# Decoder layer on one core: three small loads held behind a weight's cast, attention and decay steps shifted, cross-attention's scores in float32r parts

## The chip, the cores and the metric

The kernel runs on one core of one Trainium2 chip, in one launch. The metric is the device time of one execution in microseconds (us). The core has five engines that run side by side: TensorE (PE in the profile, with its weight loads as PEld), VectorE (DVE), ScalarE (ACT), GpSimd (POOL) and SyncE (SP). Each engine runs its own instructions strictly in order, and waits on semaphores for the others. Loads and stores are issued by SP, ACT or POOL and carried out by 16 DMA engines.

## The reference

One hybrid decoder layer on 256 tokens of width 2048, all in float32:

```
x = x + 0.5 * swiglu(rms_norm(x), ffn1)                     # inner width 5632
p = rms_norm(x) @ w_in;  q, k, v, p_rwkv, gates = split(p)
y_attn = sliding_window_attention(q, k, v, sinks)           # 16 heads, 4 kv heads, window 128
y_rwkv = rwkv7_time_mix(p_rwkv, ...)                        # 16 heads of 64
x = x + (gate_a * (y_attn @ w_pa) + gate_r * (y_rwkv @ w_pr)) @ w_out
x = x + cross_attention(rms_norm(x), rms_norm(mem)) @ w_o   # 4 heads of 128, 256 memory rows
x = rms_norm(x + 0.5 * swiglu(rms_norm(x), ffn2))
```

The attention has a learned sink per head, which enters the maximum and the denominator of the softmax: `p = e / (sum(e) + exp(sink - m))`. In the RWKV part a decay and a rate come from sigmoids of two small products, and the state is updated token by token; the kernel computes it in blocks, with the inverse of a triangular matrix per head and block. In cross-attention the scores are `s = q km^T / sqrt(128)` for each of 4 heads, then a softmax over the 256 rows of the memory. Every matrix product has to keep float32's accuracy, more or less.

## The kernel before

Nearly all of the time goes to products of 256 tokens with the weights. A weight tile (128 rows, 2 blocks of rows, 512 columns) is loaded by SP into a buffer `raw`. ACT casts it to the shorter type float32r (`hi`, line 345), DVE subtracts to get the rest (`lo`, line 346), and PE runs three float32r matmuls of 128x512 in place of one float32 matmul: hi times the activations' hi (line 438), lo times hi (439) and hi times the activations' lo (440). I call these the big matmuls. The two feed-forward blocks also save products by sums and differences of weight tiles (lines 365 to 371).

Everything else is woven between the big matmuls. Each such piece of work is a Python generator: `attend` for sliding-window attention, `decay_and_rate`, `removal_keys`, `substitute`, `invert` and `chain` for RWKV, `look_up` for cross-attention, `late_vectors` for small constants. After every six big matmuls `product` calls `bg.tick()`, which advances each generator at the head of its group by one step, up to its next `yield`. `yield from idle(n)` skips n ticks. So the numbers in `idle` set where a piece's instructions enter the program. After that a scheduler may still move instructions of an engine forward or back where data allow; `tc.issue_after(i)` forbids moving ahead of the instruction i. `newest["act"]` is the latest cast of a weight.

The parts that the change touches:

- `late_vectors` loads three small arrays from POOL: later gains (32 KB, line 266), the RWKV vectors (41.5 KB, line 267) and the sinks (8 KB, line 268), and derives `nk_k` and `ok_a` from the second on DVE (lines 270, 271). It waits 60 ticks first, but its loads have nothing to wait for.
- `attend(kvs, qb)` runs six times: scores (line 179, PE), maximum (964, DVE), exponentials (970, ACT, one for each head), denominators (977 to 979, DVE), scaling (980, DVE), transposes by PE (187), a copy `pt` (996, ACT) and the product with the values (179). `kvs` are the key-value heads, `qb` the block of 128 queries.
- `decay_and_rate` has two halves of eight sigmoids each (line 1109, ACT), and pauses after each. `tok` (line 907, ACT) is the scaled result of a projection, which PE then transposes (187).
- `substitute` inverts small blocks row by row and stores them twice with POOL (`xd` line 1254, `xe` 1256), the second after a transposing copy on ACT (1255). `invert` loads them as `xb` and `xu` (lines 1341, 1345), and joins the blocks by small matmuls (1351), at its last level through a copy `n2_` (1388).
- `look_up` multiplies `qc` and `km` for cross-attention's scores (line 1693), in float32. The profile shows each such matmul as two records.

Of the kernel before, what the change touches and what calls it, by code (L numbers as in the profile page):

```python
# [15 lines left out]
P = 128  # L16
# [126 lines left out]
def decoder_layer(ctx: ExitStack, tc: tile.TileContext, a: dict, out: bass.AP):  # L143
# [19 lines left out]
    def f32(x):  # L163
        return x.bitcast(F32)
# [28 lines left out]
    def idle(n):  # L193
        for _ in range(n):
            yield
# [67 lines left out]

    def late_vectors():
        yield from idle(60)
        pool.dma_start(gains[:], a["g_later"])
        pool.dma_start(rv[:], a["v_rwkv"])
        pool.dma_start(sinks[:], a["attn_sinks"].broadcast_to([P, 16]))
        yield from idle(20)
        dve.tensor_scalar(nk_k[:], k_k, -1.0, None, ALU.mult)  # L270
        dve.tensor_scalar(ok_a[:], k_a, -1.0, 1.0, ALU.mult, ALU.add)
# [384 lines left out]
    def feats(tok, cols=(0, P, 2 * P, 3 * P)):  # L656


        b = two()[:].rearrange("p a (c t) -> p (a c) t", t=T)
        turn(  # L660
            (b[:, i, t * P : (t + 1) * P], tok[:, t, col : col + P])
            for t in (1, 0) for i, col in enumerate(cols)
        )
        return b[:, : len(cols)]
# [227 lines left out]
    with tc.tile_pool(name="mx", bufs=1, reuse_waits="tile") as sp:  # L892
        aligned(sp)

        def t4(name, shape=(P, 4, T), dt=F32):
            return sp.tile(list(shape), dt, tag="t4", name=name, bufs=N4)
# [14 lines left out]


        def to_features(tok, dst, name):
            last = act.copy(dst[:], feats(tok))
            if name == "q0":
                with tc.issue_after(last.ins):
                    act.activation(junk_t[:, :1], ones[:, :1], AF.Exp)
            yield
            bg.seen.add(name)
# [4 lines left out]
        def attend(kvs, qb):  # L924
# [27 lines left out]
            def each(name):  # L952
                return stat.tile([P, n], F32, tag=name, name=name)
# [2 lines left out]
                return v[:].rearrange("p (e k c) -> p e k c", e=2, k=nk)  # L956

            m, nm, es, den = (each(name) for name in ("m", "nm", "es", "den"))
            b3 = b[:].rearrange("p e (c w) -> p (e c) w", w=w)
            s3 = s[:].rearrange("p e c w -> p (e c) w")  # L960
            sink = sinks[:, 4 * kvs[0] : 4 * kvs[0] + n].rearrange(
# [18 lines left out]
            dve.tensor_tensor(  # L980
                s3, s3, den[:].unsqueeze(2).to_broadcast([P, n, w]), ALU.mult
            )
            yield from idle(5 if nk == 2 and kvs[0] else 4)
            pt = t4("pt", (P, 2, 4, P))
            b = two()
            turn(
# [97 lines left out]
        def decay_and_rate():  # L1084
            yield from wait_for("small")
            yield from wait_for("attn")
            wa = t4("wa", (P, RW))
            pool.dma_start(wa[0:64, :], W["rwkv_w2"])
            pool.dma_start(wa[64:128, :], W["rwkv_a2"])
            act.activation(xwa[0:64, :], xwa[0:64, :], AF.Tanh)  # L1090
            act.activation(xg, xg, AF.Sigmoid)
            yield from idle(3)
            for h in range(2):
                cs.append(t4("cs"))
                aa.append(t4("aa"))
                for q in (0, 2):
                    b = two()
                    by_turns(
                        (
                            b[:, e, i * T : (i + 1) * T],  # L1100
                            wa[64 * e : 64 * e + 64, (4 * h + q + i) * P : (4 * h + q + i + 1) * P],
                            xwa[64 * e : 64 * e + 64, :],
                        )
                        for i in range(2) for e in (1, 0)
                    )
                    for i in range(2):
                        for e, (dst, bias) in enumerate(((cs[h], w0), (aa[h], a0))):
                            c = 4 * h + q + i
                            rates = act.activation(
                                dst[:, q + i, :], b[:, e, i * T : (i + 1) * T], AF.Sigmoid,  # L1110
                                bias=bias[:, c : c + 1],
                            )
                yield from idle(4)
            for h in range(2):
                for c in range(4):
                    dve.tensor_tensor_scan(
                        cs[h][:, c, :], keep2, cs[h][:, c, :], 0.0, ALU.mult, ALU.add
                    )
                    if c % 2:
                        yield  # L1120
                c3 = halves(cs[h])
                mid = stat.tile([P, 8], F32, tag="mid", name="mid")
                dve.tensor_copy(mid[:], c3[:, :, 63])
                dve.tensor_tensor(
                    c3, c3, mid[:].unsqueeze(2).to_broadcast([P, 8, P]), ALU.subtract
                )
                dec.append(stat.tile([P, 4], F32, tag="dec", name="dec"))
                dve.tensor_tensor(dec[h][:], cs[h][:, :, 127], mid[:, 1:8:2], ALU.add)
                yield
                ee.append(t4("ee", (P, 8, P)))  # L1130
                e0.append(stat.tile([P, 8], F32, tag="e0", name="e0"))
                with tc.issue_after(rates.ins):
                    act.activation(dec[h][:], dec[h][:], AF.Exp, scale=-DECAY)
                    act.activation(e0[h][:], mid[:], AF.Exp, scale=DECAY)
                    act.activation(ee[h][:], c3, AF.Exp, scale=-DECAY)
                yield
                act.activation(cs[h][:], cs[h][:], AF.Exp, scale=DECAY)
                yield
            bg.seen.add("decay")
# [95 lines left out]
        def substitute():  # L1235
            yield from idle(4)
            dl = t4("dl", (P, 32, 32))
            for i in range(4):
                q = slice(32 * i, 32 * i + 32)
                pool.dma_start(dl[q], ld[q, :, q].rearrange("t h s -> h t s"))  # L1240
            xt = t4("xt", (P, 32, 32))
            pool.memset(xt[:], 0.0)
            pool.memset(xt[:].rearrange("p u t -> p (u t)")[:, 0 : 32 * 32 : 33], 1.0)
            yield from idle(14)
            tmp = t4("tmp", (P, 32, 32))
            for t in range(1, 32):
                dve.tensor_tensor(
                    tmp[:, :t, :t], xt[:, :t, :t],
                    dl[:, t, :t].unsqueeze(1).to_broadcast([P, t, t]), ALU.mult,
                )  # L1250
                yield
                dve.tensor_reduce(xt[:, :t, t], tmp[:, :t, :t], AX.X, ALU.add)
                yield from idle(1 + t // 20)
            pool.dma_start(xd[:].rearrange("i h u t -> (i h) u t"), xt[:])
            act.copy(tmp[:96], xt[:96].rearrange("p u t -> p t u"))
            pool.dma_start(xe[:].rearrange("i h t u -> (i h) t u"), tmp[:96])
            yield from idle(2)
            bg.seen.add("inverse")
# [68 lines left out]
        def invert(h):  # L1327
# [58 lines left out]
                for c, n in both  # L1386
            )
            act.copy(n2_[low].rearrange("p c n t -> p c (n t)"), b[low])
            yield
            b = two()  # L1390
            several(
                (b[low, c, n * 64 : n * 64 + 64], xu[low, c, n, :], n2_[low, c, n, :])
# [279 lines left out]
                bg.spawn("mem", memory())  # L1672


        km, vm, qc = t4("km"), t4("vm", (P, 2, 512)), t4("qc")
        bg.until(lambda: hasattr(nm_, "r"))
        tok = scaled(product(nm_.x, W["w_cross_kv"]), nm_.r)
        bg.spawn("feat", to_features(tok, km, "km"))
# [5 lines left out]
        def look_up(t):  # L1684
            yield from wait_for("qc")
            ts = slice(t * P, (t + 1) * P)
            s = t4("sm")
            m = stat.tile([P, 4], F32, tag="m", name="m")
            nm = stat.tile([P, 4], F32, tag="nm", name="nm")
            den = stat.tile([P, 4], F32, tag="den", name="den")  # L1690
            b4 = two()[:].rearrange("p a (h m) -> p (a h) m", h=2)
            for h in range(4):
                pe.matmul(b4[:, h], qc[:, h, ts], km[:, h, :], start=True, stop=True)
            dve.tensor_reduce(m[:], b4, AX.X, ALU.max)
            dve.tensor_scalar(nm[:], m[:], -SC, None, ALU.mult)
            for h in range(4):
                act.activation(
                    s[:, h, :], b4[:, h, :], AF.Exp, scale=SC, bias=nm[:, h : h + 1],
                    accum_out=den[:, h : h + 1],
                )  # L1700
            yield
            dve.reciprocal(den[:], den[:])
            for i in range(4):
                dve.tensor_scalar(s[:, i, :], s[:, i, :], den[:, i : i + 1], None, ALU.mult)
            yield
            b = two()
            turn(
                (b[:, mb, i * P : (i + 1) * P], s[:, i, mb * P : (mb + 1) * P])
                for i in (3, 2, 1, 0) for mb in range(2)
            )  # L1710
            for mb in range(2):
                act.copy(pt[mb][:, :, ts], b[:, mb].rearrange("p (h t) -> p h t", h=4))
            yield
# [141 lines left out]
```

## Time and profile before

| what | value |
|---|---|
| median of 3 runs | 2218.01 us (2217.72 to 2218.32) |
| the profiled execution's own time | 2218.37 us |
| its span (first to last instruction) | 2216.6 us |
| mean granted TensorE clock | 0.999 |
| busy: PE / PEld / DVE / ACT / POOL | 2202.8 / 1816.7 / 1761.8 / 1197.5 / 72.2 us |
| moved by DMA | 433.31 MB, mean 195 GB/s |

The busy times are of the profiled execution. Its own time exceeds its span by 1.8 us, which lies around the first and the last instruction. PE's records overlap: a big matmul lasts 0.39 us in the trace, and the next one starts 0.23 us after it. So distances from start to start tell more about PE than durations. In a row of the timeline stand the start, the duration, the engine, the line, the operation with its output and inputs, the number of instructions that follow each other, and in square brackets the idle time ahead of it with the instruction that ended it. In a row of the chain stand the start and the duration of a piece of the chain of work that ended last.

Stages in the trace: the first feed-forward block until about 690 us, then the input projection with attention at about 765 to 825, RWKV's decay at about 845 to 855, its inversion and chain until 1200, the output projection, cross-attention at about 1440 to 1470, and the second feed-forward block until the end.

### The profile page before, as it was taken

The page shows a single profiled execution, that of the slowest core. Times are in us where ns is not written, and L with a number is a line of the kernel's source. Part 1 is how long each engine was busy: PE and PEld are TensorE (multiplying, and loading weights), DVE is VectorE, ACT ScalarE, POOL GpSimd, SP SyncE. Part 2 cuts the span into 40 slices and gives each one's busy share as a digit, 9 for nine tenths or more (in the row PEclk, how much of TensorE's full clock was granted, in tenths as well). Part 3 has the DMA queues.
Part 4 walks back from the last instruction along what each step waited for, and adds up shares of the span by engine and source line. Part 5 has one row for each costly group of instructions (what it writes and reads, how often), then busy time and mean ns, then how long its engine had stood idle before and what let it go on. Part 6 is the DMA issues. An engine that isn't in the chain of part 4 may idle for free.

```text
span 2216.6 us, 28327 instructions
## 1 busy us (share of the span) xinstructions
PE 2202.8 (99%) x10774; PEld 1816.7 (82%) x10774; DVE 1761.8 (79%) x2053; ACT 1197.5 (54%) x1447; POOL 72.2 (3%) x141
## 2 busy tenths in 40 slices
PE   9999999999999999999999999999999999999998
PEld 7888888888888877888888888888888888888886
DVE  8988988898887477888556676558888988898887
ACT  6555555555555557534445455556555555555554
POOL 1000000000000000010400000000000000000000
PEclk9999999999999999999999999999999999999999
DMA  7665665565656545677714765557565565565564
GB/s 261 205 219 194 204 207 192 190 209 190 209 178 220 171 128 155 214 230 222 206 54 150 235 218 202 184 171 262 193 206 185 196 209 191 188 209 196 203 207 153
DMA packets 220536, 433.31 MB, mean 195 GB/s; under 512 B 13952, under 2 KB 16336, under 8 KB 220400
## 3 DMA queue, kind: packets, MB, share of 16 engines
q1 hardware_dynamic: 213200, 410.70, 56.0%
q0 software_dynamic: 6624, 20.14, 2.9%
q8 instruction: 84, 1.38, 0.2%
q10 hardware_dynamic: 576, 0.66, 0.1%
q14 instruction: 52, 0.43, 0.1%
HBM read 419.00 MB, written 12.45 MB: 195 GB/s over the span
## 4 chain that ended last, share of the span: by engine, by line
PE 96%; DVE 1%; DMA 1%; ACT 1%; issue 1%; SPq 0%; POOLq 0%; POOL 0%; ACTq 0%; DVEq 0%
PE acc L438 21%; PE acc L439 21%; PE acc L440 21%; PE two L438 9%; PE two L439 9%; PE two L440 9%; PE two L187 2%; PE two L179 1%; DMA raw<-in_ffn_w_up_dram 1%; DVE lo L346 1%; PE two L1351 0%; PE acc L1488 0%; PE acc L1453 0%; PE acc L1470 0%; PE acc L1351 0%
## 5 line engine op out<-in xcount | busy, mean ns | idle before, releaser
L345 ACT CAST hi<-raw 128x1024 fp32r<-128x1024 f32 (+1 forms) x769 | 762.8, 1001 | 791.8 <-PE two L440 370.5
L346 DVE TENSOR_TENSOR lo<-raw,hi 128x1024 fp32r<-128x1024 f32 (+1 forms) x770 | 884.3, 1158 | 321.2 <-ACT hi L345 320.0
L438 PE MATMUL acc<-hi,xhi 128*128 128x512 f32 (+1 forms) x1224 | 478.1, 391 | 1.2 <-ACT hi L345 0.8
L439 PE MATMUL acc<-lo,xhi 128*128 128x512 f32 (+1 forms) x1224 | 475.2, 388 | 1.3 <-DVE lo L346 1.3
L440 PE MATMUL acc<-hi,xlo 128*128 128x512 f32 (+1 forms) x1224 | 474.3, 388 | 0.0
L438 PEld LDWEIGHTS acc<-hi,xhi 128*128 128x128 f32 x1224 | 229.7, 188 | 52.9 <-issue 3.9
L439 PEld LDWEIGHTS acc<-lo,xhi 128*128 128x128 f32 x1224 | 230.0, 188 | 49.5 <-DVE lo L346 3.7
L440 PEld LDWEIGHTS acc<-hi,xlo 128*128 128x128 f32 x1224 | 229.9, 188 | 46.4 <-DVE xlo L712 0.2
L371 DVE TENSOR_TENSOR tlo<-raw,thi 128x1024 fp32r<-128x1024 f32 x160 | 193.1, 1221 | 0.0
L370 ACT CAST thi<-raw 128x1024 fp32r<-128x1024 f32 x160 | 165.7, 1050 | 33.3 <-DVE raw L365 18.8
L439 PE MATMUL acc<-lo,hhi 128*128 128x512 f32 x424 | 166.5, 393 | 0.0
L440 PE MATMUL acc<-hi,hlo 128*128 128x512 f32 x424 | 165.3, 390 | 0.0
L438 PE MATMUL acc<-hi,hhi 128*128 128x512 f32 x424 | 160.0, 391 | 0.1
L438 PE MATMUL two<-hi,xhi 128*128 128x512 f32 x352 | 138.5, 393 | 0.0
L439 PE MATMUL two<-lo,xhi 128*128 128x512 f32 x352 | 137.3, 390 | 0.0
L440 PE MATMUL two<-hi,xlo 128*128 128x512 f32 x352 | 137.2, 390 | 0.0
L365 DVE TENSOR_TENSOR raw<-raw 128x1024 f32<-128x1024 f32 x80 | 97.6, 1220 | 13.7 <-DMA raw<-in_ffn_w_up_dram 13.1
L439 PEld LDWEIGHTS acc<-lo,hhi 128*128 128x128 f32 x424 | 79.6, 188 | 19.0 <-DVE lo L346 2.9
L438 PEld LDWEIGHTS acc<-hi,hhi 128*128 128x128 f32 x424 | 79.2, 188 | 18.8 <-ACT hi L345 2.6
L440 PEld LDWEIGHTS acc<-hi,hlo 128*128 128x128 f32 x424 | 79.6, 188 | 16.2
L438 PEld LDWEIGHTS two<-hi,xhi 128*128 128x128 f32 x352 | 66.1, 188 | 14.7 <-DVE u L590 0.2
L440 PEld LDWEIGHTS two<-hi,xlo 128*128 128x128 f32 x352 | 66.1, 188 | 13.8
(403 smaller groups left out, 3199.0 us busy)
## 6 DMA issues: line engine op xcount, KB each, us to landing
raw<-in_ffn_w_gate_dram SPq DMA_DIRECT2D x171, 512.0 KB, 3.7
raw<-in_ffn_w_up_dram SPq DMA_DIRECT2D x167, 512.0 KB, 4.6
raw<-in_ffn_w_down_dram SPq DMA_DIRECT2D x152, 512.0 KB, 4.6
raw<-in_w_in_dram SPq DMA_DIRECT2D x136, 512.0 KB, 3.5
raw<-in_w_out_dram SPq DMA_DIRECT2D x32, 512.0 KB, 3.6
raw<-in_ffn_w_down_dram SPq DMA_DIRECT2D x12, 1024.0 KB, 5.0
raw<-in_w_proj_attn_dram SPq DMA_DIRECT2D x16, 512.0 KB, 3.5
raw<-in_w_proj_rwkv_dram SPq DMA_DIRECT2D x16, 512.0 KB, 4.3
```

Source lines behind the costliest of these rows:

```text
L179: prev = pe.matmul(to, lhs, rhs, **how)
L187: prev = pe.transpose(to, src, ident[:])
L345: newest["act"] = act.copy(hi[:, s], raw[:, s])
L346: newest["dve"] = dve.tensor_tensor(lo[:, s], raw[:, s], f32(hi[:, s]), ALU.subtract)
L365: dve.tensor_tensor(ta[:], raw[:, 1:3], raw[:, 0:2], ALU.subtract)
L370: act.copy(hi[:, s], t[:])
L371: dve.tensor_tensor(lo[:, s], t[:], f32(hi[:, s]), ALU.subtract)
L438: pe.matmul(o, xh, hi, start=first, stop=False, **how)
L439: pe.matmul(o, xh, lo, start=False, stop=False, **how)
L440: newest["pe"] = pe.matmul(o, xl, hi, start=False, stop=last, **how)
```

## The change

It has five parts. (1) `late_vectors` writes a single column of each of its three target tiles with ACT, ordered behind the newest weight's cast. The three loads overwrite these columns, so they have to wait for ACT. (2) `attend` skips two more ticks ahead of the maximum for one call (second query block, first key-value head), and the number of ticks ahead of the transposes becomes 6 for the last two calls of the second query block, and 4 for the others, one of which had 5. (3) `decay_and_rate` skips 7 ticks instead of 4 after each half. (4) `substitute` splits its transposing copy into two with a tick between, and `invert` skips two ticks instead of one ahead of the last product of its first half. (5) `km` and `qc` become pairs of float32r parts, made by ACT's copy and a DVE subtraction, and each score is three float32r matmuls instead of one in float32.

```diff
     def late_vectors():
         yield from idle(60)
+        with tc.issue_after(newest["act"].ins):
+            for v in (gains, rv, sinks):
+                act.activation(v[:, :1], g_ffn1[:, :1], AF.Copy)
         pool.dma_start(gains[:], a["g_later"])
...
         def to_features(tok, dst, name):
-            last = act.copy(dst[:], feats(tok))
+            src = feats(tok)
+            if isinstance(dst, list):
+                act.copy(dst[0][:], src)
+                dve.tensor_tensor(dst[1][:], src, f32(dst[0][:]), ALU.subtract)
+            else:
+                last = act.copy(dst[:], src)
...
             m, nm, es, den = (each(name) for name in ("m", "nm", "es", "den"))
+            if qb and not kvs[0]:
+                yield from idle(2)
...
-            yield from idle(5 if nk == 2 and kvs[0] else 4)
+            yield from idle(6 if kvs[0] > 1 else 4)
...
-                yield from idle(4)
+                yield from idle(7)
...
-            act.copy(tmp[:96], xt[:96].rearrange("p u t -> p t u"))
+            for t in (slice(0, 16), slice(16, 32)):
+                act.copy(tmp[:96, t], xt[:96, :, t].rearrange("p u t -> p t u"))
+                yield
...
             act.copy(n2_[low].rearrange("p c n t -> p c (n t)"), b[low])
-            yield
+            yield from idle(2 - h)
...
-        km, vm, qc = t4("km"), t4("vm", (P, 2, 512)), t4("qc")
+        km, qc = ([t4(n, dt=F32R) for _ in range(2)] for n in ("km", "qc"))
+        vm = t4("vm", (P, 2, 512))
...
-                pe.matmul(b4[:, h], qc[:, h, ts], km[:, h, :], start=True, stop=True)
+                for i, j in ((0, 0), (0, 1), (1, 0)):
+                    pe.matmul(
+                        b4[:, h], qc[i][:, h, ts], km[j][:, h, :],
+                        start=h % 2 + i + j == 0, stop=i == 1, skip_group_check=True,
+                    )
```

What the change does to the order of instructions is seen at three places. The first is DVE during the first two calls of attention, from the denominators on; `den` and `s` with 8 columns belong to the first call, those with 4 to the second, and `lo` is a weight's low part. Before:

```order
L977 TENSOR_REDUCE den<-s 128x8
L977 TENSOR_REDUCE den<-s 128x4
L346 TENSOR_TENSOR lo<-raw,hi 128x1024
L978 TENSOR_TENSOR den<-den,es 128x8
L978 TENSOR_TENSOR den<-den,es 128x4
L346 TENSOR_TENSOR lo<-raw,hi 128x1024
L979 RECIPROCAL den<-den 128x8
L979 RECIPROCAL den<-den 128x4
L346 TENSOR_TENSOR lo<-raw,hi 128x1024
L980 TENSOR_TENSOR s<-s,den 128x1024 x2
```

With the change, whose line numbers are 3 to 10 higher here:

```order
L987 TENSOR_REDUCE den<-s 128x8
L349 TENSOR_TENSOR lo<-raw,hi 128x1024
L988 TENSOR_TENSOR den<-den,es 128x8
L989 RECIPROCAL den<-den 128x8
L987 TENSOR_REDUCE den<-s 128x4
L990 TENSOR_TENSOR s<-s,den 128x1024
L349 TENSOR_TENSOR lo<-raw,hi 128x1024
L988 TENSOR_TENSOR den<-den,es 128x4
L349 TENSOR_TENSOR lo<-raw,hi 128x1024
L989 RECIPROCAL den<-den 128x4
L990 TENSOR_TENSOR s<-s,den 128x1024
```

The first weight part now stands behind one reduction instead of two, and the first call's scaling stands ahead of two weight parts that it stood behind. In the same place ACT has its cast for this weight part behind the first call's eight exponentials and ahead of the second call's four, where it was behind all twelve; and PE has 42 big matmuls instead of 52 between the scores and the first transposes.

The second place is ACT at the second half of the sigmoids in `decay_and_rate`; `tok` is a projection's result for 128 tokens. Before:

```order
L1109 ACTIVATE cs<-two,v_rwkv 128x256
L1109 ACTIVATE aa<-two,v_rwkv 128x256
L907 ACTIVATE tok<-acc,rs 128x512
L1109 ACTIVATE cs<-two,v_rwkv 128x256
L1109 ACTIVATE aa<-two,v_rwkv 128x256
L1109 ACTIVATE cs<-two,v_rwkv 128x256
L1109 ACTIVATE aa<-two,v_rwkv 128x256
L907 ACTIVATE tok<-acc,rs 128x512
```

With the change:

```order
L910 ACTIVATE tok<-acc,rs 128x512 x2
L348 CAST hi<-raw 128x1024
L1064 COPY p<-two 128x4x256
L348 CAST hi<-raw 128x1024 x2
L1119 ACTIVATE cs<-two,v_rwkv 128x256
L1119 ACTIVATE aa<-two,v_rwkv 128x256
```

Both token halves now come ahead of all eight sigmoids of the second half, with three casts between. On POOL, the two loads of `wa` for these products (lines 1088 and 1089) now stand behind the second clearing of a column of `p` (line 1053), which they stood ahead of; PE's first product with `wa` comes 19 big matmuls later, counted from the transposes of `tok` ahead of it.

The third place is PE at cross-attention's scores. Before:

```order
L438 MATMUL acc<-hi,mehi 128x512
L439 MATMUL acc<-lo,mehi 128x512
L440 MATMUL acc<-hi,melo 128x512
L1693 MATMUL two<-km,qc 128x256 x8
L438 MATMUL acc<-hi,mehi 128x512
```

With the change:

```order
L443 MATMUL acc<-hi,melo 128x512
L1707 MATMUL two<-km,qc 128x256 x2
L441 MATMUL acc<-hi,mehi 128x512
L442 MATMUL acc<-lo,mehi 128x512
L443 MATMUL acc<-hi,melo 128x512
L441 MATMUL acc<-hi,mehi 128x512
L1707 MATMUL two<-km,qc 128x256 x22
```

The eight float32 matmuls are 24 in float32r. The first two, which need no low part of `qc`, come ahead of four big ones, and the other 22 follow.

## The prediction, made before the result was known

> **What bounds the kernel now.** I read the page first: busy times and the chain that ended last.
>
> ```profile
> span 2216.6 us, 28327 instructions
> PE 2202.8 (99%) x10774; PEld 1816.7 (82%) x10774; DVE 1761.8 (79%) x2053; ACT 1197.5 (54%) x1447; POOL 72.2 (3%) x141
> PE 96%; DVE 1%; DMA 1%; ACT 1%; issue 1%; SPq 0%; POOLq 0%; POOL 0%; ACTq 0%; DVEq 0%
> ```
>
> TensorE is busy for 2202.8 of 2216.6 us and is 96% of the chain. So an edit can win only in two ways: by taking matmul time away, or by closing one of the short holes in PE's row. Work on DVE, ACT or a queue counts only where PE waits for it. The waits of PE, grouped by who ends them (total, times, longest), name the holes; the costliest are for weights' low parts:
>
> ```profile
> PE acc L439 <- DVE lo L346: 1.3, 4, 0.6
> ```
>
> A wait is shorter in that view than what PE loses. The PE timeline at the longest of them shows by how much (start, duration, then the idle time before it and its releaser):
>
> ```profile
> 776.61 0.39 PE L440 MATMUL acc<-hi,xlo 128*128 128x512 f32 x1
> 776.84 0.39 PE L438 MATMUL acc<-hi,xhi 128*128 128x512 f32 x1
> 777.83 0.50 PE L439 MATMUL acc<-lo,xhi 128*128 128x512 f32 x1 [0.60 <-DVE lo L346]
> ```
>
> Matmuls follow each other every 0.23 us although each lasts 0.39. From 776.84 to 777.83 is 0.99, so the loss is 0.99 - 0.23 = 0.76: the bracket plus 0.16. I add 0.16 to each bracket below.
>
> **Edit 1, the three small loads.** Before, they issue at the very start:
>
> ```profile
> 6.14 10.16 DMA raw<-in_ffn_w_up_dram
> 12.06 0.73 PE L438 MATMUL acc<-hi,xhi 128*128 128x512 f32 x2 [0.56 <-ACT hi L345]
> 13.32 0.50 PE L439 MATMUL acc<-lo,xhi 128*128 128x512 f32 x1 [0.29 <-DVE lo L346]
> 18.76 0.50 PE L439 MATMUL acc<-lo,xhi 128*128 128x512 f32 x1 [0.18 <-DVE lo L346]
> ...
> 5.93 0.73 POOL L266 DMA_DIRECT2D g_later<-in_g_later_dram  x1
> ...
> q1 hardware_dynamic: 7396, 14.79, 71.0%
> q0 software_dynamic: 96, 0.08, 1.2%
> v_rwkv<-in_v_rwkv_dram POOLq DMA_DIRECT2D x1, 41.5 KB, 5.3
> ```
>
> The chain's longest early piece is a weight tile that takes 10.16 us to land, and three holes follow it: 0.72 + 0.45 + 0.34 = 1.51 us. The small loads are all of queue q0 in the first 60 us: 1.2% of 60 is 0.72 us of all 16 engines' time, in the stretch where the weights arrive. Without them each weight tile behind lands earlier. Bounds: 0 (the packets fill gaps between others) and 1.51 (all three holes close). I take 0.5, under the 0.72 since not every packet stands ahead of the tile that PE waits for. Per MB q0 costs 0.72/0.08 = 9 us and q1 42.6/14.79 = 2.9.
>
> The Trainium skill, "DMA: Bandwidth & Descriptors", section Specifications, has 512 B as the least piece that moves at line rate; smaller ones are read, modified and written. The rows agree (three times the time per MB). By bytes alone at q1's 2.9 the loads would be 0.23 us, by the queue's own time 0.72.
>
> What the edit adds: three ACT copies of 128x1, a wait on POOL, and two DVE operations that now stand far later.
>
> ```profile
> 774.90 0.28 ACT L975 ACTIVATE es<-es 128x4 f32<-128x4 f32 x1
> ...
> 96.03 0.72 ACT L584 ACTIVATE hb<-hb,rs 128x512 f32<-128x512 f32 x1 [1.48 <-DVE hb L583]
> 111.78 0.69 DVE L367 TENSOR_TENSOR raw<-raw,raw 128x512 f32<-128x512 f32 x1
> ```
>
> In the new order ACT's copies stand just ahead of this L584, with 1.48 us idle there; three of them, at 0.28 each like L975's 128x4, fit in. Cost 0. On POOL the loads wait until about 95, after the power of L756 which formerly ran at 39, and the next entry behind them is a store of far later rows: nobody waits. They land by about 95 + 0.7 + 6 = 102; DVE reaches the two vector operations at 111.7, just ahead of this L367. Cost 0, with 10 us in hand; if that cover were gone, DVE and all weight parts behind it would wait one for one.
>
> **Edit 2, attention.** Four holes, A to D, in order of time.
>
> ```profile
> 774.30 2.35 DVE L977 TENSOR_REDUCE den<-s 128x8 f32<-128x1024 f32 x2 [2.82 <-ACT s L970]
> 776.56 1.21 DVE L346 TENSOR_TENSOR lo<-raw,hi 128x1024 fp32r<-128x1024 f32 x1
> ...
> 781.16 0.39 PE L438 MATMUL acc<-hi,xhi 128*128 128x512 f32 x1
> 781.61 1.06 PE L187 MATMUL two<-ident,s 128*128 128x128 f32 x8
> ...
> 818.29 0.52 PE L187 MATMUL two<-ident,s 128*128 128x128 f32 x3 [0.61 <-DVE s L980]
> ...
> 850.14 0.50 ACT L1109 ACTIVATE cs<-two,v_rwkv 128x256 f32<-128x256 f32 x1
> 851.57 0.75 ACT L907 ACTIVATE tok<-acc,rs 128x512 f32<-128x512 f32 x1
> 852.37 0.88 PE L187 MATMUL two<-ident,tok 128*128 128x128 f32 x6 [0.44 <-ACT tok L907]
> ```
>
> A (0.76, at 777.83): the weight's low part, 776.56 to 777.77, waits behind two reductions of 2.35 / 2 = 1.18. In the new order only one stands ahead of it, and four of ACT's exponentials stand behind the cast. So the low part ends by 777.77 - 1.18 = 776.6, and PE wants it at 776.84 + 0.23 = 777.07: closed, with half a us in hand.
>
> B (0.45 - 0.23 = 0.22, at 781.61): the first transposes are 42 big matmuls after the scores where they were 52. PE would be there at 781.39 - 10 x 0.23 - 0.76 (A's hole) = 778.3. DVE runs reduction, weight part, reduction and scaling ahead of them, 4 x 1.18 and some 0.2 of small operations, 4.9 us; with the four exponentials (about 0.7 us) out of the way it starts near 773.6 and ends at 778.5. So a hole of 0.1 to 0.2 stays; I take a gain of 0.1, bounds -0.5 (the exponentials don't help and DVE ends at 779.0) and 0.22.
>
> C (0.61 + 0.16 = 0.77, at 818.29): in the new order the scaling L980 goes ahead of two weight parts of 1.2 us each, and the transposes come six small matmuls later. It closes.
>
> D (0.44 + 0.16 = 0.60, at 852.37): the second token half waits on ACT behind sigmoids. With the longer pause between the halves, both token halves now stand ahead of the second half's eight sigmoids, as the order in the section on the change shows. From 850.14 to 851.57 four sigmoids run on ACT, 1.43 us by which the token half starts sooner: it closes.
>
> Together 0.76 + 0.1 + 0.77 + 0.60 = 2.2. Bounds: 2.35 if all close; below, a hole that closes can reopen one step on, since a weight part follows in each of these queues. If each reopens at half its size, 1.2.
>
> **Edits 3 and 4, decay steps and inversion.** The longer pause moves keys, inversion and chain some 36 to 66 big matmuls (8 to 15 us) later against the projections.
>
> ```profile
> 860.00:1090.00 230.00, 230.00 (x1073) 190.00 (x1072) 184.18 (x220) 118.30 (x124) 36.97 (x61) 1.00 0.71 216
> 1090.00:1200.00 110.00, 109.56 (x1193) 93.53 (x1192) 61.28 (x61) 47.58 (x65) 7.79 (x16) 1.00 0.31 97
> 1111.25 2.08 PE L1351 MATMUL two<-n,xu 64*64 64x64 f32 x32 [0.21 <-ACT n L1388]
> 1030.47 2.15 ACT L1255 COPY tmp<-xt 96x1024 f32<-96x1024 f32 x1 [0.48 <-DVE xt L1252]
> ```
>
> (The first two rows are stretches: bounds, length, busy time of PE, PEld, DVE, ACT and POOL.) The stretch of the inversion's last levels and the chain, 1090 to 1200, has 110.00 - 109.56 = 0.44 us idle; with 0.16 for each of some four holes PE loses about 1.1 there. One hole has a clear cure: at 1111.25 PE waits for the copy n2_, 0.21 + 0.16 = 0.37, and the pause of two steps at h = 0 puts two more big matmuls (0.46) ahead. The others, such as PE behind DVE's products for the chain, are reshuffled and may stay. I take 0.4; bounds 1.1, and -1.2 if one more full-width DVE operation comes uncovered. Splitting the 2.15 us copy at 1030.47 lets a cast in between: PE has no hole there (230.00 busy of 230.00). The copy's cover is that idle-free PE: gain 0, and the later store costs 0 since PE's first reader moves 15 us later as well. A switch between big and small matmuls has a price too, but the order has as many as before, give or take one: cost 0.
>
> **Edit 5, cross-attention's scores.**
>
> ```profile
> 1450.64 3.62 PE L1693 MATMUL two<-km,qc 128*128 128x256 f32 x16
> 1454.32 0.40 PE L439 MATMUL acc<-lo,mehi 128*128 128x512 f32 x1
> ...
> 1458.88 0.39 PE L438 MATMUL acc<-hi,mehi 128*128 128x512 f32 x1
> 1459.33 0.84 PE L187 MATMUL two<-ident,sm 128*128 128x128 f32 x6
> ...
> 1199.46 1.90 PE two L1593 x16
> ...
> 1449.46 1.02 ACT L914 COPY qc<-two 128x1024 f32<-128x1024 f32 x1 [0.61 <-PE two L187]
> 1451.92 1.22 DVE L346 TENSOR_TENSOR lo<-raw,hi 128x1024 fp32r<-128x1024 f32 x1 [1.81 <-ACT hi L345]
> ```
>
> Eight fp32 matmuls, recorded as 16, stand with one big one between 1450.64 and 1454.32: 3.68, less 0.23 for the big one 3.45 us. The nearest row for the new form is L1593, float32r of 128x256: 16 in 1.90, or 0.119 each. Twenty-four take 2.85, so 0.60 less. (The Trainium skill, "FP8 and Floating Point Precision", section TensorE Precision Notes, counts four passes for true fp32. Three for four would make 3.45 into 2.59, 0.86 less; by the row it is 0.60, since 3.45 / 8 = 0.43 per fp32 matmul is only 3.6 times 0.119.)
>
> The price is two DVE subtractions of 1.2 us. That of qc can start after ACT's 1450.48 and ends near 1451.72, just as L346 of 1451.92 gets its cast, so the weight part isn't delayed. PE runs two score matmuls and four big ones first (0.24 + 0.92), and wants the low part at about 1451.8: no wait, or a few hundredths. The softmax hole, (1459.33 - 1458.88) - 0.23 = 0.22, is filled by transposes that come three big matmuls later; 0.1 of it goes. Sum 0.70; bounds 0.82 (0.60 and the whole hole) and -0.5 (0.70 less one DVE operation of 1.2 late).
>
> **Sum.** 0.5 + 2.2 + 0.4 + 0.7 = 3.8. A profiled execution of 2218.37 becomes 2214.6; its time lies 0.36 above the median of 2218.01, so for a median of runs I write 2214.2. I call a change within 0.2%, 4.4 us, not to be told from none: below 2213.6 is faster, above 2222.4 slower.
>
> **Rivals.** (1) Everything at its upper bound: 1.51 + 2.35 + 1.1 + 0.82 = 5.8; with the start whole and the rest as forecast, 4.8. Time 2218.0 less 5.3, their middle, 2212.7, faster. For it: the start is one coupled chain in which an earlier tile closes all three holes, and q0's packets are dearer than their bytes. Against: 0.72 us of queue can't easily give 1.51. Chance 0.30. (2) The holes move on: A to D reopen at half, the chain gives 0, the start gives 0. With cross-attention's 0.7 this makes 1.2 + 0.7 = 1.9, time 2216.1, same. For it: DVE is busy for 79% and weight parts stand in the same queue. Against: PE has half a us in hand at A, and 1.43 - 0.60 = 0.8 at D. Chance 0.17. (3) Slower: `wa`, the weights of the decay's two small products, comes too late. Place: POOL, where its loads stood ahead of the clearing of a column of p (L1053) and now stand behind it.
>
> ```profile
> 787.05 0.57 POOL L1088 DMA_DIRECT2D wa<-in_rwkv_w_dram  x1 [60.23 <-PE acc L179]
> ...
> 829.68 0.11 POOL L1053 MEMSET p<- 128x4 f32 x1 [41.53 <-DVE xs L1061]
> 839.31 0.92 PE L179 MATMUL two<-xs,wa 64*128 64x256 f32 x6
> ```
>
> The clearing waits for DVE's xs until 829.68. So the loads go from 787 to about 829.8, the second lands near 829.8 + 2 x 0.57 + 5.3 (as v_rwkv) = 836.2. PE read them at 839.31; in the new order 19 more big matmuls stand ahead (4.3 us), less the 2.1 of A, B, C: 841.5. In hand are 5.3 us, so I forecast no wait. Beyond that PE waits one for one, since nothing else stands ready behind this matmul in its queue; to be slower by 0.2% the loads must be 5.3 + 3.8 + 4.4 = 13.5 us later still, time 2222.5 and up. Against it: DVE's xs moves by one or two operations of 1.2 us in the new order, not by ten. Chance 0.04.
>
> **How the numbers follow.** Forecast 0.49, rivals 0.30, 0.17, 0.04. Faster 0.33 (rival 1, and a little of the forecast's edge), slower 0.04, within 0.2% the rest, 0.63. The range: low end 2212.2, which is all of rival 1's 5.8; high end 2217.2, which takes in rival 2 and the 1.2 by which its cross term may fail (0.7 to -0.5).
>
> **What would show it.** Right: PE's waits lose L980's and tok's rows and one of the lo; the L1707 rows take near 2.85 us; the first 20 us lose about 1 us of holes and the POOL loads stand near 95. Wrong: a PE wait of over 0.3 us near 776, 817 or 852 for another releaser (edit 2 merely moved it), a PE wait on wa, xb or xu, holes of the same size before 20 us with the loads gone (they never mattered), or a PE wait on DVE qc.

## The result, and the profile after

| | before | with the change |
|---|---|---|
| median of 22 runs each | 2218.36 us | 2215.33 us (2214.43 to 2216.02) |
| the profiled execution's own time | 2218.37 us | 2215.92 us |
| its span | 2216.6 us | 2214.2 us |

The ratio is 0.9986, with a 95% interval of 0.998 to 0.9992: 3.0 us or 0.14% less. That is within the 0.2% that I had called not to be told from none, though the interval lies wholly below 1. The prediction said 2214.2 in 2212.2 to 2217.2, with "within 0.2%" the likeliest.

The profile's page, and the waits of PE in the changed kernel:

```profile
span 2214.2 us, 28352 instructions
PE 2202.0 (99%) x10782; PEld 1815.2 (82%) x10782; DVE 1764.9 (80%) x2055; ACT 1198.8 (54%) x1451; POOL 71.7 (3%) x141
PE 96%; DVE 2%; DMA 1%; ACT 0%; issue 0%; SPq 0%; POOLq 0%; POOL 0%; ACTq 0%; DVEq 0%
...
PE acc L442 <- DVE lo L349: 0.5, 2, 0.3
PE two L187 <- ACT tok L910: 0.2, 1, 0.2
PE two L187 <- DVE s L990: 0.2, 1, 0.2
```

PE is still 96% of the chain. Waits for low parts fell from 1.3 us to 0.5, and the waits for `s` and `tok` are smaller but not gone. To see where the time went I count PE's big matmuls, 8976 in each kernel, and compare the start of the same one in two profiles. Each row says by how much that difference changed over the stretch; a negative number means that time was gained against the profile before:

| stretch of the profile before | forecast | the change | the change again (e10) |
|---|---|---|---|
| start, until 21 us (61st big matmul) | -0.5 | -0.42 | -0.50 |
| rest of the first feed-forward block and start of the input projection, to 752 us | 0 | +1.03 | +0.07 |
| attention and decay, to 967 us | -2.2 | -1.66 | -1.63 |
| inversion and chain, to 1249 us | -0.4 | -0.48 | -0.47 |
| output projection and cross-attention, to 1468 us | -0.7 | -0.47 | -0.46 |
| second feed-forward block, to 2208 us | 0 | -0.46 | -0.42 |

The three middle rows agree within 0.03 us between the two profiles, so they are the change's. The second and the last row, mostly feed-forward, come and go in kernels with and without the change: from 21 to 752 us the profiles lose 0 to 1.18 us with the loads at the start and 0.07 to 1.03 with them held, 0.45 on the mean of each. A single profile therefore decides nothing about the start; there I use all profiles.

In the middle, these are the holes that the changed kernel has and why. PE's rows first, then the DVE and ACT rows that PE waited for:

```profile
778.58 0.39 PE L443 MATMUL acc<-hi,xlo 128*128 128x512 f32 x1
779.20 1.06 PE L187 MATMUL two<-ident,s 128*128 128x128 f32 x8 [0.23 <-DVE s L990]
...
821.26 0.88 PE L187 MATMUL two<-ident,tok 128*128 128x128 f32 x6 [0.24 <-ACT tok L910]
...
958.51 1.16 PE L179 MATMUL two<-kk,at 64*128 64x128 f32 x16
```

```profile
775.30 1.22 DVE L349 TENSOR_TENSOR lo<-raw,hi 128x1024 fp32r<-128x1024 f32 x1
...
776.75 1.17 DVE L987 TENSOR_REDUCE den<-s 128x4 f32<-128x1024 f32 x1
777.84 1.22 DVE L990 TENSOR_TENSOR s<-s,den 128x1024 f32<-128x1024 f32 x1
...
957.14 1.22 DVE L1210 TENSOR_TENSOR kk<-kk,cs 128x1024 f32<-128x1024 f32 x1
...
819.58 0.84 ACT L980 ACTIVATE s<-two,nm 128x256 f32<-128x256 f32 x2 [0.24 <-DVE nm L976]
820.32 0.89 ACT L910 ACTIVATE tok<-acc,rs 128x288 f32<-128x288 f32 x2
```

Hole A is closed: the low part is ready at 776.52. B grew from 0.22 to 0.39 us: DVE's scaling ends at 779.06, and PE would have started the transposes 0.39 us earlier than it did. C is closed, but PE now comes to the transposes of `tok` early and waits 0.40 us, where two exponentials stand ahead of `tok` on ACT. Near 958 is a new hole of 0.28 us: PE comes to the product of keys while DVE still makes `kk` (until 958.36). D is closed.

### The profile page after: what moved, and what is told of

Read it like the earlier page. It is cut to its first block, busy times and chain, and to the rows that moved or that the text cites. A ratio compares the mean times of both kernels' runs of the same rounds, so it can differ in the third digit from the quotient of the medians.

```text
span 2214.2 us, 28352 instructions
## 1 busy us (share of the span) xinstructions
PE 2202.0 (99%) x10782; PEld 1815.2 (82%) x10782; DVE 1764.9 (80%) x2055; ACT 1198.8 (54%) x1451; POOL 71.7 (3%) x141
## 4 chain that ended last, share of the span: by engine, by line
PE 96%; DVE 2%; DMA 1%; ACT 0%; issue 0%; SPq 0%; POOLq 0%; POOL 0%; ACTq 0%; DVEq 0%
PE acc L441 21%; PE acc L442 21%; PE acc L443 21%; PE two L441 9%; PE two L442 9%; PE two L443 9%; PE two L187 2%; PE two L179 1%; DVE lo L349 1%; DMA raw<-in_ffn_w_up_dram 1%; PE two L1363 0%; PE acc L1500 0%; PE acc L1482 0%; PE acc L1465 0%; PE acc L179 0%
```

## The experiments

Each has its own 10 or 11 runs and 33 runs of the kernel before on the same chip, in groups of four kernels.

| run | median, us | before, us | ratio, 95% interval |
|---|---|---|---|
| e1 loads held | 2218.74 | 2218.95 | 1.0 (0.9991 to 1.0009) |
| e2 attention's steps | 2217.66 | 2218.95 | 0.9997 (0.9988 to 1.0005) |
| e34 decay, inversion | 2216.83 | 2218.95 | 0.9991 (0.9982 to 1.0) |
| e5 cross-attention | 2218.37 | 2218.95 | 0.9997 (0.9988 to 1.0005) |
| e6 loads twice | 2221.85 | 2219.09 | 1.001 (1.0001 to 1.0019) |
| e7 attention, split copy | 2217.60 | 2219.09 | 0.9991 (0.9982 to 1.0) |
| e8 whole, unsplit | 2215.12 | 2219.09 | 0.9982 (0.9973 to 0.9991) |
| e9 decay alone | 2218.32 | 2219.09 | 0.9994 (0.9985 to 1.0003) |
| e10 whole again | 2215.38 | 2218.68 | 0.9984 (0.9975 to 0.9992) |
| e11 whole, unsplit again | 2214.41 | 2218.68 | 0.9982 (0.9973 to 0.999) |
| e12 unsplit, tok and keys | 2215.40 | 2218.68 | 0.9987 (0.9978 to 0.9996) |
| e13 unsplit, three holes | 2215.23 | 2218.68 | 0.9985 (0.9976 to 0.9994) |

Single medians don't tell parts of half a us apart; the traces do, and what follows rests on them.

### The small loads alone, and twice (e1, e6)

```diff
     def late_vectors():
         yield from idle(60)
+        with tc.issue_after(newest["act"].ins):
+            for v in (gains, rv, sinks):
+                act.activation(v[:, :1], g_ffn1[:, :1], AF.Copy)
```

> The kernel before with part 1 alone: the three small loads held behind a weight's cast. Theory (the packets delay the weights at the start): the hole near 18.2 us (0.34 us) is gone, the ones near 11 and 12.6 us stay, 0.4 to 0.5 us less in all. Rival (the packets fill gaps): all three holes stay, time within 0.1 us of before. A second question is on record with it: the profile of the whole change showed two new holes near 88 and 97 us (0.35 and 0.20 us). If the held loads cause them, they are here again and eat the gain; if a weight tile's landing merely varies, they are absent.

e6 leaves the loads where they were, and adds a second set:

```diff
         pool.dma_start(sinks[:], a["attn_sinks"].broadcast_to([P, 16]))
+        for v, name in ((gains, "g_later"), (rv, "v_rwkv")):
+            again = cpool.tile(list(v.shape), F32, name=f"{name}_2")
+            pool.dma_start(again[:], a[name])
+        for i in range(3):
+            again = cpool.tile([P, 16], F32, name=f"sinks_{i}")
+            pool.dma_start(again[:], a["attn_sinks"].broadcast_to([P, 16]))
```

> The kernel before with the suspected cost doubled: a second copy of each of the two larger small loads, and three more of the sinks, all issued by POOL behind the first three into tiles that nothing reads. Theory (packets of these loads delay the weights): PE's sixtieth big matmul, near 21 us, comes 0.4 to 0.7 us later than in the kernels with the loads once, with the hole near 18 us at 0.5 us or more. Rival (the start varies by itself, 0.35 us earlier to 1.05 later in the profiles so far, and the loads have no part): within that spread, and no longer time.

The start of the 61st big matmul, against the profile before (21.41 us), in every profile taken:

| loads | profiles | mean | tile issued near 6 us lands at | hole near 18 us |
|---|---|---|---|---|
| at the start | 0, -0.39, -0.20, +0.60, +1.17 (before, e2, e5, e7, e34) | +0.24 | 15.91 to 17.45, mean 16.53 | 0.22 to 0.80 us, in 5 of 5 |
| held | -0.42, -0.49, +0.02, -0.50, -0.30, -1.00, -0.97 (the change, e1, e8, e10 to e13) | -0.52 | 14.34 to 15.37, mean 14.83 | none, in 7 of 7 |
| twice | +2.09 (e6) | | 18.41 | 1.5 and 1.0 us |

(e9, with its loads at the start, is left out: its matmuls ran at a lower clock there, see the end. Its tile landed at 17.59, and it has no hole near 18 us.) Between the first two rows lie 0.76 us. The kernels ran on several chips; e6's own has e7 at +0.60 and e8 at +0.02. First e6: the early tile in its chain, PE's waits, and the DMA queue of the small loads in the first 60 us. Then the changed kernel: the early tile in its chain, which is now an earlier one, PE's waits, and the first of the held loads:

```profile
6.12 12.29 DMA raw<-in_ffn_w_up_dram
...
13.16 0.50 PE L445 MATMUL acc<-lo,xhi 128*128 128x512 f32 x1 [0.30 <-DVE lo L352]
19.61 0.49 PE L444 MATMUL acc<-hi,xhi 128*128 128x512 f32 x1 [1.37 <-ACT hi L351]
20.87 0.50 PE L445 MATMUL acc<-lo,xhi 128*128 128x512 f32 x1 [0.77 <-DVE lo L352]
...
q0 software_dynamic: 256, 0.18, 5.3%
```

```profile
4.28 6.66 DMA raw<-in_ffn_w_up_dram
...
12.12 0.73 PE L441 MATMUL acc<-hi,xhi 128*128 128x512 f32 x2 [0.54 <-ACT hi L348]
13.38 0.50 PE L442 MATMUL acc<-lo,xhi 128*128 128x512 f32 x1 [0.30 <-DVE lo L349]
...
95.17 0.73 POOL L269 DMA_DIRECT2D g_later<-in_g_later_dram  x1 [55.86 <-ACT sinks L268]
```

So the packets do delay the weights: take them away and the hole near 18 us goes, double them and it becomes 2.5 us. The landings show it without overlap: on the mean the tile comes 1.70 us later with the loads once than with them held (16.53 and 14.83), and 3.58 later with them twice, about as 0.08 MB stands to 0.18. PE loses less by the first dose, 0.76 us, since it doesn't wait for the tile when that comes early; it loses the second one for one, 1.85 us for 1.88, where I had expected 0.4 to 0.7. The tile issued near 4.3 us, ahead of the small loads, lands at 10.56 to 11.55 us with the loads at the start and at 10.35 to 11.37 with them held, so the holes near 12 and 13 us stay. The queue's own time grows by more than the bytes, from 0.72 to 3.2 us of all 16 engines (5.3% of 60); why was not separated.

e1's median shows only 0.2 us of the gain. Its profile has the 0.49 us at the start, lost 0.56 again by 752 us, within the spread of that stretch, and 0.8 behind 1613 us, mostly to a low part near 1653 us, a hole that varies from profile to profile. The two holes near 88 and 97 us are absent in e1 and present in e34, which has no held loads: the held loads don't cause them.

### Attention's steps alone, and with the split copy (e2, e7)

```diff
             m, nm, es, den = (each(name) for name in ("m", "nm", "es", "den"))
+            if qb and not kvs[0]:
+                yield from idle(2)
...
-            yield from idle(5 if nk == 2 and kvs[0] else 4)
+            yield from idle(6 if kvs[0] > 1 else 4)
```

> The kernel before with part 2 alone: the shifted steps of the sliding-window attention. Theory: holes A (0.76 us near 777) and C (0.77 near 817) close, B (0.22 near 781) becomes 0.2 to 0.4 by DVE's scaling, D (0.60 near 851) stays since it belongs to the decay's pause: 1.2 to 1.5 us less. Rival (the holes move on): each of A and C reopens at half its size, 0.6 to 0.8 us less.

A and C closed, B was 0.39, and the 0.39 us wait for `tok` near 820 is here too, so both come from this part. D closed as well, which I had not expected of it: the decay starts when attention is done, and moved with it. What neither theory had, either: a hole of 1.47 us far behind, near 1033. PE, and ACT ahead of it, in e2:

```profile
1034.87 0.33 PE L187 MATMUL two<-ident,tok 128*128 128x128 f32 x1 [1.31 <-ACT tok L907]
...
1031.53 2.13 ACT L1257 COPY tmp<-xt 96x1024 f32<-96x1024 f32 x1 [0.95 <-DVE xt L1254]
1033.56 1.26 ACT L907 ACTIVATE tok<-acc,rs 128x512 f32<-128x512 f32 x2
```

Before, the copy of `substitute` stood ahead of this projection's `tok` too, but ended at 1032.62, 0.84 us before `tok` began. Attention's shifted steps moved it later, and now `tok` waits behind it. e7 adds the split of that copy:

```diff
-            act.copy(tmp[:96], xt[:96].rearrange("p u t -> p t u"))
+            for t in (slice(0, 16), slice(16, 32)):
+                act.copy(tmp[:96, t], xt[:96, :, t].rearrange("p u t -> p t u"))
+                yield
```

> Part 2 with the split transposing copy. With part 2 alone PE waited 1.47 us near 1033 for tok, which stood behind the unsplit copy of 2.13 us on ACT. Theory (the split is there to let tok in between): that hole falls by about one half copy, 1.1 us, to 0.3 or 0.4. Rival (tok is late for another reason): the hole stays above 1.2 us.

My theory falls. The hole stayed, at 1.41 us (the rival had it above 1.2), and ACT's rows show why:

```profile
1033.04 1.17 ACT L1258 COPY tmp<-xt 96x512 f32<-96x512 f32 x1 [0.87 <-DVE xt L1254]
1034.10 0.69 ACT L907 ACTIVATE tok<-acc,rs 128x512 f32<-128x512 f32 x1
1034.68 1.07 ACT L1258 COPY tmp<-xt 96x512 f32<-96x512 f32 x1
1035.65 0.69 ACT L907 ACTIVATE tok<-acc,rs 128x512 f32<-128x512 f32 x1
```

PE needs both halves of `tok`, and the second still stands behind both halves of the copy. A split helps only if all that is waited for gets in between.

### The decay's pause, with part 4 and alone (e34, e9)

e34 is parts 3 and 4 of the change; e9 is only

```diff
-                yield from idle(4)
+                yield from idle(7)
             for h in range(2):
                 for c in range(4):
```

> The kernel before with parts 3 and 4 alone: the longer pause in the decay, the split copy, the longer pause before the inversion's last product. Theory: D (0.60 us) closes, and the hole behind n2_ (0.38) closes, other holes of the chain stay: 0.8 to 1.0 us less. Rival (the chain meets new holes after its shift): less than 0.5 us.

> The kernel before with part 3 alone, the decay's longer pause. Theory: hole D (0.60 us near 851) closes by this alone; the hole behind n2_ (0.38 near 1110) stays, since its pause is part 4; a hole of 0.3 to 0.6 us near 1053, which the run of parts 3 and 4 had, stays if the pause causes it. Net 0.0 to 0.4 us less than before between 750 and 1250 us. Rival (the shift of the chain closes n2_'s hole, not its own pause): 0.38 is gone here too.

Between 752 and 1249 us, e34 gained 1.14 us and e9 1.35, where I had expected 0.8 to 1.0 and at most 0.4. D closed in both (and in e2: either part is enough). The hole behind `n2_` (0.38) closed in e9 as well, and in e2, which both lack part 4: a shift closed it, as the rival had it, and not the second tick ahead of the product. e34's hole of 0.55 us near 1053 is not in e9, so there it comes with part 4 and not from the pause.

### Cross-attention's scores alone (e5)

```diff
-                pe.matmul(b4[:, h], qc[:, h, ts], km[:, h, :], start=True, stop=True)
+                for i, j in ((0, 0), (0, 1), (1, 0)):
+                    pe.matmul(
+                        b4[:, h], qc[i][:, h, ts], km[j][:, h, :],
+                        start=h % 2 + i + j == 0, stop=i == 1, skip_group_check=True,
+                    )
```

> The kernel before with part 5 alone: cross-attention's scores in float32r parts. Theory: 24 matmuls of 0.119 us for 3.45 us, 0.60 less, and the softmax hole stays at 0.2: 0.5 to 0.7 us less. Rival (four passes become three): 0.86 less and more. Second rival (DVE's subtraction for qc comes late): a hole of some tenths ahead of the 22 score matmuls, gain below 0.4.

Between 1415 and 1468 us e5 gained 0.44 us, as the whole change did. The rows of the change (PE, then DVE), and the maximum in the kernel before:

```profile
1449.10 0.40 PE L1707 MATMUL two<-km,qc 128*128 128x256 f32 x2
1450.26 2.88 PE L1707 MATMUL two<-km,qc 128*128 128x256 f32 x22
1452.98 0.40 PE L442 MATMUL acc<-lo,mehi 128*128 128x512 f32 x1
1457.54 0.39 PE L441 MATMUL acc<-hi,mehi 128*128 128x512 f32 x1
1458.01 1.06 PE L187 MATMUL two<-ident,sm 128*128 128x128 f32 x8
...
1448.97 1.23 DVE L920 TENSOR_TENSOR qc<-two,qc 128x1024 fp32r<-128x1024 f32 x1 [0.41 <-ACT qc L919]
1451.74 1.23 DVE L1711 TENSOR_REDUCE m<-two 128x4 f32<-128x1024 f32 x1
```

```profile
1453.06 1.22 DVE L1694 TENSOR_REDUCE m<-two 128x4 f32<-128x1024 f32 x1
```

Twenty-two matmuls take 1452.98 - 1450.26 = 2.72 us, 0.124 each where L1593 took 0.119. With 0.24 for the first two that is 2.96 for 3.45: 0.49 gained instead of 0.60. The low part of `qc` ends at 1450.20, just ahead of the 22: no wait, as forecast. But the softmax hole stayed, 1458.01 - 1457.54 - 0.23 = 0.24. PE has three big matmuls more ahead of the transposes (0.69 us), but the shorter scores bring it there 0.49 sooner: counted from the first score matmul it arrives after 8.67 us instead of 8.47. And the maximum starts after 2.64 us instead of 2.42 (1453.06 against 1450.64), since four big matmuls now stand between the first two score matmuls and the rest. That eats the 0.20. The Trainium skill, "FP8 and Floating Point Precision", section TensorE Precision Notes, counts four passes for true fp32, which would have made the gain 0.86 us; the rows give 0.49.

### The whole change unsplit (e8, e10, e11)

e8 and e11 are the whole change without part 4's split copy:

```diff
-            for t in (slice(0, 16), slice(16, 32)):
-                act.copy(tmp[:96, t], xt[:96, :, t].rearrange("p u t -> p t u"))
-                yield
+            act.copy(tmp[:96], xt[:96].rearrange("p u t -> p t u"))
```

> The whole change with the transposing copy in one piece again. In the whole change ACT's tok stands ahead of the copy and PE has no hole there. Theory (the split matters only where tok stands behind it): no new hole near 1030 to 1045, time as the whole change within 0.2 us. Rival (the split gives the whole change a part of its gain): a hole of 0.5 to 1.5 us near 1040.

> The whole change once more, beside the next three on the same chip. Theory: 3.0 us less than before, as in its first 22 runs; in its profile the same six holes behind the middle of the layer (0.39 near 778, 0.40 near 820, 0.28 near 958, 0.23 and 0.28 near 1130, 0.24 before the transposes of cross-attention), since they come from the order of instructions; the holes before 100 us differ from its first profile, since they come from landing times.

> The whole change with the transposing copy in one piece, once more beside it. Theory (the split costs 0.8 us: the stretch from 1060 to 1249 us was 0.82 shorter without it): 0.6 to 1.0 us less than the whole change on the same chip. Rival (the difference was between chips): within 0.3 us of it.

No hole came near 1040, as expected, for in the whole change `tok` is long done when the copies run. But the time wasn't the same: between 967 and 1249 us e8 gained 1.30 us against the profile before, and the whole change 0.48. Side by side, e11 is 0.97 us under e10 (2214.41 and 2215.38), with 1.26 and 0.47 in that stretch. So this edit costs the whole change 0.8 us, and the unsplit version is the fastest kernel here, 4.0 (e8) and 4.3 us (e11) under before. Where the 0.8 lies is settled only in part: 0.28 is the hole in front of the chain's product with `mk` near 1131, which the unsplit version doesn't have. The rest is spread, in pieces of at most 0.2 us, over transitions between small matmuls that stand in another order; both have the same 501 big and 1056 small matmuls and 48 switches between them from 1060 to 1249 us. With attention's steps alone, the same split gained 0.77 us (e7 against e2, 752 to 1249 us). Its worth depends on what else has moved.

That the two pieces of the copy cost the 0.8 us is not shown, for the edit also adds two steps, which move all that follows. From 1060 to 1249 us PE takes 187.7 to 188.0 us in e7, e34, e8 and e11, and 188.4 to 189.2 in the kernel before, e2, e9, the whole change, e12 and e13 (both below). Each of the two groups has kernels with the copy whole and with the copy in two, so it is rather the place of the chain's steps that counts. A kernel with the two steps and the whole copy was not run.

e10's holes were those of the first profile: 0.40, 0.40, 0.28, 0.23, 0.28 and 0.25 us, at the same places.

### Two more holes attacked (e12, e13)

On the unsplit version, e12:

```diff
-            if qb and not kvs[0]:
-                yield from idle(2)
+            if qb and kvs[0] in (0, 3):
+                yield from idle(1 if kvs[0] else 2)
...
             dve.tensor_tensor(aa[h][:], kt[h][:], ei[:], ALU.mult)
+            yield
             for c in range(2):
```

and e13, in addition:

```diff
-            yield from idle(6 if kvs[0] > 1 else 4)
+            yield from idle(6 if kvs[0] > 1 else 4 if kvs[0] or qb else 5)
```

> The unsplit version with two holes attacked: the maximum of the last attention call waits one tick more, so that tok (the 0.40 us hole near 820) goes ahead of its exponentials on ACT, and the product of keys waits one tick more for DVE (the 0.28 us hole near 958). Theory (a hole closes if its piece moves by a tick): both gone, 0.5 to 0.7 us less than the unsplit version. Rival (a shift of all later pieces makes new holes of the same size): within 0.3 us of it, with new holes between 820 and 1200.

> As the one before, and the first attention call's transposes one tick later, against the 0.39 us hole near 778 where PE waits for DVE's scaling. Theory: that hole goes too, 0.9 to 1.1 us less than the unsplit version. Rival (both first calls then meet, and a later call has its hole instead): no better than the one before.

Both theories fell. The 0.40 and 0.28 us holes went, but the times were 1.0 and 0.8 us over e11: worse than e12's rival had it, which kept within 0.3 us, and e13 is only 0.2 under e12. In e12 hole D is back at its full 0.60 us, and so is the chain's `mk` hole (0.28). That attention ends a tick later, and the decay with it, would explain D; it was not tested apart. PE and ACT in e12:

```profile
847.75 1.09 PE L187 MATMUL two<-ident,tok 128*128 128x128 f32 x8 [0.44 <-ACT tok L910]
...
846.59 0.53 ACT L1119 ACTIVATE aa<-two,v_rwkv 128x256 f32<-128x256 f32 x1
846.95 0.75 ACT L910 ACTIVATE tok<-acc,rs 128x512 f32<-128x512 f32 x1
```

These four holes add up to 0.20 us of loss, but from 752 to 1249 us e12 lost 0.91 against e11. Of that, 0.79 lie behind 967 us: with the copy whole, e12's shifted steps cost the chain what the split copy cost it, and beyond the `mk` hole the loss is again spread. In e13 B didn't close but grew to 0.48, D is back as well, and one of 0.31 for `pt` came near 804.

## Why the prediction was right, and where its steps were off

- **The whole**: 3.0 us measured, 3.8 forecast, the right class and inside the range. The terms by the traces are 0.76 + 1.65 + 0.48 + 0.46 = 3.35; the medians gave 3.03 and, in e10, 3.30. (The range's high end is worked out a little short: 2216.1 and 1.2 make 2217.3.)
- **Start**: forecast 0.5. The mechanism holds (e6, and the landings), and the hole near 18 us went in all seven profiles. The mean over profiles is 0.76, with single profiles up to 0.9 us off their group's mean. One reading was wrong: three holes do not follow the tile that takes 10.16 us. Issued at 6.14, it landed at 16.30, behind the holes at 12.06 and 13.32. Only the third could follow it, and only the third closed. The late copies cost nothing: ACT idled there, the vectors landed by 102 us, and DVE passed `nk_k` at 112.15 without a wait.
- **Attention and decay**: forecast 2.2, measured 1.65; this is the term that was mis-sized. A and D closed as worked out. B was to shrink by 0.1 and grew by 0.17. DVE's scaling ended 0.25 us behind PE's arrival (779.06 against 778.81), close to the 0.2 worked out; left out were the 0.14 us from DVE's end to PE's start. C's step, "It closes", looked only at DVE; PE then came sooner to `tok`, whose wait C had covered, and 0.40 of the 0.77 went there. The shift of the keys brought 0.28 more near 958. Together that makes 0.76 - 0.17 + 0.77 - 0.40 + 0.60 - 0.28 = 1.28. The other 0.37 of the 1.65 is spread over transitions between unlike matmuls in the new order, which the forecast didn't have; to that extent the term was luck. What went to new waits is rival 2 in part: a hole moves to the next thing that had been hidden behind it.
- **Inversion and chain**: forecast 0.4, measured 0.48, right in size and wrong in cause: luck. That "the pause of two steps at h = 0" puts two more big matmuls ahead isn't needed to cure the wait for `n2_`: the decay's pause alone does it (e9), and attention's steps alone (e2). And the split copy with its two steps, which I had at 0, costs 0.8 in this kernel. Part 3, which I had priced by D, brought more, and part 4 took some of it back.
- **Cross-attention**: forecast 0.7, measured 0.46; 0.124 us per matmul instead of 0.119, and none of the softmax hole, since the sum for the hole left out that PE comes there sooner by its own gain.
- **Rival 3** was far off. POOL's loads of `wa` went late, as forecast, and PE passed with 9.7 us in hand between 833.1 (828.92 and the 4.2 us that its landing took) and 842.83; I had worked out 5.3:

```profile
828.92 0.53 POOL L1099 DMA_DIRECT2D wa<-in_rwkv_a_dram  x1
842.83 2.00 PE L179 MATMUL two<-xs,wa 64*128 64x256 f32 x16
```

- **Rival 1** needed every hole at its upper bound. The start came near it in some profiles, the attention didn't.

## What to carry to other kernels

Where one engine is busy for 99%, list its holes, and for each say not only what closes it but what that hole had been hiding: the engine arrives earlier at its next wait, and the closed 0.77 us became a 0.40 us wait one piece further on. When pieces are woven by counts of steps, each shift reorders all later pieces too, so gains don't add up and a part can change its sign with its neighbours (the split copy with its two steps: 0.8 us gained in one setting, 0.8 lost in another); try removing each part from the finished whole. A small load into a busy start isn't free: 0.08 MB put off the weight tile issued beside it by 1.70 us, and the hole behind that tile is in none of the 7 profiles with the loads held. Before counting a hole as the effect of a late load, compare the two times: a hole that comes before the landing has another cause.

## What I had not expected of the hardware

In e9's profile PE ran slower for a short while at the start, in the midst of steady work. The view is busy time by stretch, with the granted clock third from the end:

```profile
10.00:14.00 4.00, 2.69 (x12) 1.71 (x10) 0.83 (x1) 1.91 (x2) 0.00 (x0) 1.00 1.03 361
14.00:18.00 4.00, 3.71 (x10) 2.84 (x10) 3.35 (x8) 2.10 (x6) 0.00 (x0) 0.61 1.02 373
18.00:25.00 7.00, 7.00 (x31) 5.73 (x31) 5.21 (x8) 5.47 (x9) 0.00 (x0) 0.98 1.02 373
```

The granted clock is 0.61 over 14 to 18 us, behind a stretch in which PE stood still for 1.5 us at 11.7. Matmuls followed each other every 0.43 us instead of 0.23. It came in one of the 14 profiles. Its nine slow intervals, 14.78 to 18.42 us, cost about 1.6 us of the 2.28 by which e9's 61st big matmul came late. In e7, e8 and e34 PE stood still for 1.2 to 1.3 us at the same place, and in e6 for 1.5 near 18 us, and kept its clock. What decides it stays open.
